# Two accumulator tiles instead of one, and an earlier place in the order for weight blocks, in a hybrid decoder trunk

## The chip, the cores and the metric

The kernel runs on one core of one Trainium2 chip. A core has five engines that each work through a queue of their own in order: TensorE (PE) multiplies 128-row blocks and writes PSUM, VectorE (DVE) and ScalarE (ACT) do elementwise work and read PSUM, GpSimd (POOL) and SyncE (SP) mostly issue transfers. They wait for each other by semaphores. The metric is the device time of one launch in microseconds. Three runs of the kernel before took 1014.68 to 1016.35 us, with a median of 1015.87.

## The reference

Input is a sequence of 512 tokens with 1024 channels, in front of which 16 learned tokens are put (528 positions). One layer is computed:

```
u    = rmsnorm(h) * mix_norm_w
proj = u @ w_in              # pool input, z, xBC, dt, two gates
y_pool = pool_mixer(u_pool) @ w_pool_up
xBC  = silu(causal_conv4(xBC))          # x: 2048, B and C: 8 groups x 128
dt   = softplus(dt + dt_bias);  a = -exp(a_log)
y    = ssd_chunked(x, dt, a, B, C) + x * d_skip      # chunks of 128 positions
y    = group_rmsnorm(y * silu(z)) * ssd_norm_w;  y_ssd = y @ w_ssd_out
h    = h + (gate_pool * y_pool + gate_ssd * y_ssd) @ w_o
h    = h + relu(rmsnorm(h) @ w_ff1)**2 @ w_ff2
out  = rmsnorm(h)[:, 16:]
```

The scan has 32 heads of 64 channels in 8 groups. In ssd_chunked a group's positions are cut into chunks; inside a chunk y is (C B^T, masked and multiplied by exp of differences of the summed decay) times x dt, between chunks a 128x64 state per head is carried on.

## The kernel before

All products are in float32, made of three products of split operands: a number is stored as a rounded part (hi) and the rest (lo), and hi·hi, hi·lo and lo·hi are summed in PSUM. A weight block is 128x1024 floats, which is eight 128x128 tiles. block() (L115) takes tiles for it, issues the load on SP's queue (L95) into one of three raw buffers, the cast to hi on ACT (L111) and the subtraction that gives lo on DVE (L113). There are four buffers each for hi (whi) and lo (wlo); a cast waits until the matmuls that read the block four places earlier are through with its buffer. A cast and a subtraction of a full block take about 1.05 and 1.2 us.

The scan goes over the groups 0 to 7. For group g, group_proj (L529) computes the projections of B, C, two halves of x and two halves of z from u, each as eight weight tiles with 16 high and 8 low matmuls per half of the positions (proj, L207; the results are the PSUM tiles px, and pz for z), and then a convolution of four taps (conv, L433: first tap on ACT L436, the others on DVE L439, silu on ACT L441). ssd (L590) computes the scan of the group before it, interleaved with these: transposes to ptb, ptm, ptx (L605 to L618); exps of the decay on ACT (eb, L632; abc, L637, L643, L644); C B^T in pcb (L655); states in pst, copied to st0 (L666) and carried on by DVE (L671, L672); the mask multiply on DVE (L675); then po (L684) from the states and py (L690) from the chunk itself, summed by DVE to yt (L693 to L697), normed by png, rs and a reciprocal (L708 to L713). A gate block (pgp) comes with some groups.

In groups 4 to 7 the two halves of x are computed together by pair() (L492), which uses seven products of half the size instead of eight: b11, b21, t2, t1, s3, b22, t4 in this order, each of 12 matmuls of 128 rows by 264 positions (8 with hi, 4 with lo weights, L505 and L508). Their operands are blocks whip and wlop from pair_operands (L471), two products to a block, and sums of u (t0h, t0l, t1h, t1l, made by L919 and L920). The products accumulate in two banks: b11, t2, s3, t4 in bank 0, b21, t1, b22 in bank 1. After each product its bank is read out to rax or rbx, by ACT (L510 b11, L515 t2, L517 t1, L524 t4) or by DVE (L512 b21, L520 s3, L522 b22), and the next product in that bank may write it when this is done.

PSUM has eight banks of 128x512 floats. Pool psa has two buffers of two banks each (psum2, L192), pool psb four of one bank (psum1, L195), in which ptb, ptm, ptx, pcb, pst, po, py and png of the scan take turns.

After the scan come its output projection, the pooling branch, w_o and the MLP (from about 690 us on), none of whose code is touched.

What sets the order of the work is a scheduler: the program is written as generators that are woven together (weave, L728), each instruction has a priority by its place in the program, and the scheduler puts each engine's queue in an order by priority among what it takes to be ready. tc.issue_after adds an order between two instructions. tc.high_priority(n) gives what is issued under it the priority of a place n instructions sooner.

Of the kernel before, what the change touches and what calls it, by code (L numbers as in the profile page):

```python
# [19 lines left out]
HALF = L // 2  # L20
# [44 lines left out]
def kernel(ctx: ExitStack, tc, xT, x, w, fx, f1, f2, vec, fnw, out):  # L65
# [15 lines left out]
    def raw_tile(name):  # L81
        nraw[0] += 1
        if scan_raw and nraw[0] % 4 == 0:
            return scan_raw[0].tile([P, 1024], F32, tag="raw", name=name)
        return wp.tile([P, 1024], F32, tag="raw", name=name, bufs=3)

    def block_tiles():
        b = nblk[0]
        nblk[0] += 1
        return (b, raw_tile(f"raw{b}"),  # L90
                wp.tile([P, 1024], F32R, tag="whi", name=f"whi{b}"),
                wp.tile([P, 1024], F32R, tag="wlo", name=f"wlo{b}"))

    def block_load(t, c):
        nc.sync.dma_start(t[1][:, c], w[t[0], :, c])  # L95
# [5 lines left out]
    def after(*ins):  # L101
        st = ExitStack()
        for i in ins:
            if i is not None:
                st.enter_context(tc.issue_after(i.ins))
        return st

    def block_split(t, c, behind=None, cast_behind=None):
        b, raw, hi, lo = t
        with after(cast_behind):  # L110
            act.copy(hi[:, c], raw[:, c])  # L111
        with tc.issue_after(behind.ins) if behind is not None else nullcontext():
            dve.tensor_tensor(lo[:, c], raw[:, c], hi[:, c].bitcast(F32), op=ALU.subtract)  # L113

    def block(behind=None, cast_behind=None):  # L115
        t = block_tiles()
        block_load(t, slice(0, 1024))
        block_split(t, slice(0, 1024), behind, cast_behind)
        return t[2:]

    def raw_block():
# [13 lines left out]
    def units():  # L135

        while True:
            hi, lo = block()
            for j in range(NK):
                yield hi[:, j * P : (j + 1) * P], lo[:, j * P : (j + 1) * P]  # L140
# [51 lines left out]
    def psum2(name):  # L192
        return psa.tile([P, 1024], F32, tag="mm", name=name)

    def psum1(name):  # L195
        return psb.tile([P, 512], F32, tag="s", name=name)
# [155 lines left out]
    for i in range(2):  # L352
        pb = psum1(f"pb1_{i}")
        c = slice(3 * i, 3 * i + 3)
# [35 lines left out]
    for c in (slice(0, P), slice(P, W)):  # L390
        n = c.stop - c.start
# [67 lines left out]
    def factor_u(name):  # L459
        if name in ("A11", "A12", "A22"):  # L460
            o = 0 if name == "A11" else 4
            c = HF[1] if name == "A22" else HF[0]
            return [(uh[o + k][:, c], ul[o + k][:, c]) for k in range(4)]
        n, c = {"S1": ("1", HF[1]), "S2": ("0", HF[0]), "S3": ("0", HF[1]), "S4": ("1", HF[0])}[name]
        return [(T[n, "h", k][:, c], T[n, "l", k][:, c]) for k in range(4)]
# [5 lines left out]
    def pair_operands(i):  # L471

        s, h = divmod(i, 2)
        q = {"b11": B11, "b22": B22, "b21": B21}
        for a in range(0, 7, 2):
            ms = [m[0] for m in MULTIPLY[a : a + 2]]
            n = nblk[1]
            nblk[1] += 1
            raw = raw_tile(f"rawp{n}")
            hi = wp.tile([P, 1024], F32R, tag="whi", name=f"whip{n}")  # L480
            lo = wp.tile([P, 1024], F32R, tag="wlo", name=f"wlop{n}")
            for j, m in enumerate(ms):
                src = fx[s, q[m]] if m in q else wsum["fx", s, m]
                nc.sync.dma_start(raw[:, 512 * j : 512 * (j + 1)], src[:, 512 * h : 512 * (h + 1)])
            c = slice(0, 512 * len(ms))
            block_split((n, raw, hi, lo), c)
            for j in range(len(ms)):
                yield hi[:, 512 * j : 512 * (j + 1)], lo[:, 512 * j : 512 * (j + 1)]

# [1 line left out]

    def pair(kind, g, r):  # L492

        ps = psum2(f"pq{kind}{g}")
        banks = (ps[:, :HALF], ps[:, 512 : 512 + HALF])
        operands = pair_operands(PAIRS.index((kind, g)))
        one, two = HF
        for m, f, n, start, stop in MULTIPLY:
            o = banks[n]
            wt = next(operands)  # L500
            f = factor_u(f)
            for low in range(2):
                for k in range(4):
                    wk = wt[low][:, k * P : (k + 1) * P]
                    at = pe.matmul(o, wk, f[k][0], start=start and not low and k == 0,  # L505
                                   stop=stop and low == 1 and k == 3, skip_group_check=True)
                    if not low:
                        pe.matmul(o, wk, f[k][1], start=False, stop=False, skip_group_check=True)  # L508
            if m == "b11":
                act.copy(r[0][:, one], o)  # L510
            elif m == "b21":
                dve.tensor_tensor(r[0][:, one], r[0][:, one], o, op=ALU.add)  # L512
            elif m == "t2":
                second_product[g] = at
                act.activation(r[1][:, one], o, AF.Copy, scale=-1.0)  # L515
            elif m == "t1":
                act.copy(r[1][:, two], o)  # L517
                yield
            elif m == "s3":
                dve.tensor_tensor(r[1][:, two], r[1][:, two], o, op=ALU.subtract)  # L520
            elif m == "b22":
                dve.tensor_tensor(r[1][:, one], r[1][:, one], o, op=ALU.add)  # L522
            else:
                act.copy(r[0][:, two], o)  # L524
# [4 lines left out]
    def group_proj(g, cur, gate=None):  # L529
# [4 lines left out]
        def plain(dst, t, skip):  # L534
            if first and (dst is bt or dst is ct):
                view = viewB if dst is bt else viewC
            else:
                runs, view = wide(psum2(f"px{g}_{t}"), skip)
                proj(runs, block(), X if first else U)
            conv(dst, first_raw(t, view, skip) if first else view, t)  # L540

        def z_half(ps, i):

            with tc.issue_after(done[0].ins) if g == 1 else nullcontext():
                wt = block(None, halved.get(g - 1) if gate is not None else None)
            proj(narrow(ps), wt, X if first else U, None if i else second_product.get(g))
# [4 lines left out]
        for kind, ts, paired in (("b", bcs, both), ("x", xs, g in X_PAIRS)):  # L551
            if paired:
                r = raw_pair(kind, g)
                yield from pair(kind, g, r)
                for (dst, t, skip), src in zip(ts, r):
                    conv(dst, src[:, skip:], t)
                yield
            else:
                for t in ts:
                    plain(*t)  # L560
                    filled.setdefault(g - 1, mm[0])
                    yield
            if both:
                i = 0 if kind == "b" else 1
                ps = psum2(f"pz{g}_{i}")[:, :SEQ]
                z_half(ps, i)
                z_ready[g] = act.activation(zt[:, i, :], ps, AF.Silu)
                yield
# [481 lines left out]
    for d in range(NK):  # L1050
        ps = psum1(f"psl{d}")
# [108 lines left out]
    for n, d in enumerate(MERGE):  # L1160
# [9 lines left out]
        ps = psum2(f"pup{d}")[:, :SEQ]  # L1170
# [389 lines left out]
    for c in range(NC - 1):  # L1560
        z, e = c == 0, c == NC - 2

        n = 2 * c + 3
# [63 lines left out]
    c = NC - 1  # L1627
# [14 lines left out]
    for t in range(4):  # L1642
        T, st = t // 2, slice((t % 2) * P, (t % 2 + 1) * P)
        n = 0
        for half in range(2):
            parts = [(0, 512)] if half == 0 or t < 3 else [(0, 256), (256, 256)]
            for a, m in parts:
                ps = p2v[t] if T == 0 and half == 0 else lastp[:, 512:] if a else (
                    lastp[:, :512] if (t, half) == (3, 0) else psum1(f"pl{t}_{half}"))
                ps = ps[:, a : a + m]  # L1650
# [5 lines left out]
                for k, seg in ((1, (A11, 3)[T]), (0, (A12, A22)[T])):  # L1656
                    wh, wl = wq[k, half]
                    for p in range(2):
                        x0 = p * 512 + a
                        f = i == 0 and not (T == 0 and half == 0) and not a  # L1660
# [170 lines left out]
```

## Time and profile before

| | |
|---|---|
| median of three runs | 1015.87 us (1014.68 to 1016.35) |
| the profiled execution | 1013.97 us |
| its span, first to last instruction | 1012.3 us |
| TensorE busy | 992.1 us, 98% of the span |
| VectorE, ScalarE, GpSimd busy | 804.3, 604.9, 122.7 us |
| mean granted TensorE clock | 0.996 of full speed |

How to read its views: the page gives the busy time of each engine and, in 40 slices of 25.3 us, its share in tenths and the granted clock. The view of waits sums for each group of instructions how long its engine stood idle ahead of it and what ended that. The timeline lists the instructions of an engine: start, time that it or its run of like instructions took, engine, line, operation, output <- inputs by the program's names (numbers left out, so px is px3_19 or another), shapes, the count of the run, and in brackets the idle time ahead of it with its releaser. Matmuls are pipelined, so a matmul of 0.28 us may start 0.12 us after the one before it.

### The profile page before, as it was taken

What the parts mean: (1) busy time and instruction counts of PE and PEld (TensorE: products, weight loads), DVE (VectorE), ACT (ScalarE), POOL (GpSimd) and SP (SyncE); (2) the same over time, 40 slices, a digit from 0 to 9 for tenths busy, and PEclk for the clock granted to TensorE, in tenths of its full rate; (3) what the DMA queues carried; (4) which work ended last, traced back from release to release, by engine and by line L of the source; (5) the groups of instructions that cost most, each with busy time, mean ns of one, the idle gap of its engine ahead of it and who ended that gap; (6) DMA issues with size and microseconds to landing.
All of it is one profiled execution on the core that took longest, in us unless ns stands there. A gap on an engine that the chain in (4) does not pass through costs nothing.

```text
span 1012.3 us, 15679 instructions
## 1 busy us (share of the span) xinstructions
PE 992.1 (98%) x6035; PEld 874.9 (86%) x6035; DVE 804.3 (79%) x1162; ACT 604.9 (60%) x856; POOL 122.7 (12%) x215
## 2 busy tenths in 40 slices
PE   9999997999999999999999999999999999999997
PEld 7889996988888898987899888887889999999986
DVE  7968896869853788978789657876988878888885
ACT  8657848395943666675445434367656656665654
POOL 0001221211112213213300000221000000000000
PEclk9999998999999999999999999999999999999999
DMA  7274877676889758587823631989354464554432
GB/s 255 85 259 128 252 217 188 180 196 189 232 244 262 207 147 255 137 264 156 270 84 124 230 125 62 288 199 337 91 187 150 142 195 138 166 172 151 137 105 84
DMA packets 61803, 184.52 MB, mean 182 GB/s; under 512 B 7072, under 2 KB 8416, under 8 KB 60704
## 3 DMA queue, kind: packets, MB, share of 16 engines
q1 hardware_dynamic: 39456, 109.00, 32.4%
q0 software_dynamic: 18240, 67.51, 26.1%
q10 hardware_dynamic: 4032, 7.00, 1.9%
q8 instruction: 47, 0.77, 0.3%
q14 instruction: 28, 0.23, 0.1%
HBM read 173.13 MB, written 58.59 MB: 229 GB/s over the span
## 4 chain that ended last, share of the span: by engine, by line
PE 90%; ACT 5%; DVE 2%; DMA 2%; issue 1%; ACTq 0%; DVEq 0%
PE px L1450 8%; PE px L214 7%; PE alpha L1518 6%; PE pz L214 6%; PE px L1453 4%; PE px L217 4%; PE alpha L1521 3%; PE pgp L214 3%; PE pz L217 3%; PE pgs L214 3%; PE pqx L505 3%; DMA raw<-in_w 2%; PE pso L145 1%; PE pgp L217 1%; PE pso L146 1%; PE pso L148 1%
## 5 line engine op out<-in xcount | busy, mean ns | idle before, releaser
L113 DVE TENSOR_TENSOR wlo<-raw,whi 128x1024 fp32r<-128x1024 f32 (+2 forms) x88 | 101.7, 1170 | 43.7 <-ACT whi L111 25.7
L111 ACT CAST whi<-raw 128x1024 fp32r<-128x1024 f32 (+2 forms) x88 | 87.5, 1010 | 74.8 <-DMA raw<-in_w 17.8
L214 PE MATMUL px<-uh,whi 128*128 128x264 f32 (+1 forms) x320 | 82.4, 295 | 5.7 <-ACT whi L111 5.7
L217 PE MATMUL px<-ul,whi 128*128 128x264 f32 (+1 forms) x320 | 79.9, 287 | 0.0
L214 PEld LDWEIGHTS px<-uh,whi 128*128 128x128 f32 x320 | 61.5, 192 | 7.1 <-ACT whi L111 6.0
L1225 DVE TENSOR_TENSOR ht<-ht,alpha 128x1024 f32<-128x1024 f32 x35 | 42.7, 1219 | 29.1 <-PE alpha L1518 29.1
L217 PEld LDWEIGHTS px<-ul,whi 128*128 128x128 f32 x320 | 61.3, 192 | 0.2
L1148 ACT CAST shi<-rawf 128x1024 fp32r<-128x1024 f32 x42 | 44.2, 1053 | 28.6 <-PE alpha L1521 18.2
L1518 PE MATMUL alpha<-shi,hh 128*128 128x512 f32 x140 | 55.2, 394 | 0.0
L1521 PE MATMUL alpha<-shi,hl 128*128 128x512 f32 x140 | 54.7, 391 | 0.0
L1149 DVE TENSOR_TENSOR slo<-rawf,shi 128x1024 fp32r<-128x1024 f32 x42 | 51.2, 1218 | 0.6 <-ACT shi L1148 0.6
L1453 PE MATMUL px<-vsl,shi 128*128 128x256 f32 x192 | 47.4, 280 | 0.0
L1450 PE MATMUL px<-vsh,shi 128*128 128x256 f32 x192 | 47.4, 281 | 0.0
L214 PE MATMUL pz<-uh,whi 128*128 128x512 f32 x112 | 43.9, 392 | 0.0
L217 PE MATMUL pz<-ul,whi 128*128 128x512 f32 x112 | 43.7, 390 | 0.0
L214 PE MATMUL px<-uh,wlo 128*128 128x264 f32 (+1 forms) x320 | 41.8, 283 | 0.0
L214 PEld LDWEIGHTS px<-uh,wlo 128*128 128x128 f32 x320 | 39.9, 188 | 0.0
L1518 PE MATMUL alpha<-slo,hh 128*128 128x512 f32 x140 | 37.4, 389 | 0.0
L1450 PEld LDWEIGHTS px<-vsh,shi 128*128 128x128 f32 x192 | 36.2, 188 | 0.9
L1453 PEld LDWEIGHTS px<-vsl,shi 128*128 128x128 f32 x192 | 36.1, 188 | 0.9
L1453 PE MATMUL px<-vl,shi 128*128 128x256 f32 x144 | 36.1, 283 | 0.0
L713 DVE RECIPROCAL rs<-rs 128x128 f32<-128x128 f32 x32 | 27.2, 911 | 11.1 <-ACT rs L711 10.9
(593 smaller groups left out, 3079.2 us busy)
## 6 DMA issues: line engine op xcount, KB each, us to landing
raw<-in_w SPq DMA_DIRECT2D x96, 512.0 KB, 4.7
f_t<-in_f POOLq DMA_DIRECT2D x38, 512.0 KB, 6.9
f_s<-in_f POOLq DMA_DIRECT2D x26, 512.0 KB, 6.6
b<-in_f SPq DMA_DIRECT2D x21, 512.0 KB, 4.5
rawf<-in_f SPq DMA_DIRECT2D x36, 256.0 KB, 3.0
rawf<-f_t SPq DMA_DIRECT2D x36, 256.0 KB, 3.2
abc<-acs_d POOLq DMA_DIRECT2D x8, 1024.0 KB, 6.5
f_t<-f_t POOLq DMA_DIRECT2D x12, 512.0 KB, 6.7
```

Of the source, the lines that this page charges most:

```text
L111: act.copy(hi[:, c], raw[:, c])
L113: dve.tensor_tensor(lo[:, c], raw[:, c], hi[:, c].bitcast(F32), op=ALU.subtract)
L214: pe.matmul(o, wt, rhs[0][k][:, c], start=part == 0 and k == 0, stop=part == 1 and k == NK - 1)
L217: mm[0] = pe.matmul(o, wt, rhs[1][k][:, c], start=False, stop=False)
L505: at = pe.matmul(o, wk, f[k][0], start=start and not low and k == 0, stop=stop and low == 1 and k == 3, skip_group_check=True)
L1148: splits.append((act.copy(hi, src), dve.tensor_tensor(lo, src, hi.bitcast(F32), op=ALU.subtract)))
L1149: dve.tensor_tensor(lo, src, hi.bitcast(F32), op=ALU.subtract)))
L1225: added[0] = dve.tensor_tensor(o, o, src, op=op)
L1450: pe.matmul(ps, m, f[k][0], start=start and not low and k == 0, stop=stop and low == 1 and k == 3, skip_group_check=True)
L1453: pe.matmul(ps, m, f[k][1], start=False, stop=False, skip_group_check=True)
L1518: pe.matmul(ps[t], hh[:, p, seg, st], m, start=bool(first and not low and p == 0), stop=bool(last and low and p == 1), skip_group_check=True)
L1521: pe.matmul(ps[t], hl[:, p, seg, st], m, start=False, stop=False, skip_group_check=True)
```

## The change

Two edits. In block() the load and the split, and in pair_operands the split, are issued under tc.high_priority(100). In pair() bank 1 is no longer the second half of the psa tile but a psb tile of its own, pox4 to pox7; pqx4 to pqx7 stays the psa tile, of which the second bank now lies unused. No instruction is added or removed but for one table load of ACT, which falls away.

```diff
     def block(behind=None, cast_behind=None):
         t = block_tiles()
-        block_load(t, slice(0, 1024))
-        block_split(t, slice(0, 1024), behind, cast_behind)
+        with tc.high_priority(100):
+            block_load(t, slice(0, 1024))
+            block_split(t, slice(0, 1024), behind, cast_behind)
         return t[2:]
...
             c = slice(0, 512 * len(ms))
-            block_split((n, raw, hi, lo), c)
+            with tc.high_priority(100):
+                block_split((n, raw, hi, lo), c)
...
     def pair(kind, g, r):
 
-        ps = psum2(f"pq{kind}{g}")
-        banks = (ps[:, :HALF], ps[:, 512 : 512 + HALF])
+        banks = (psum2(f"pq{kind}{g}")[:, :HALF], psum1(f"po{kind}{g}")[:, :HALF])
```

Line numbers up to L116 are the same in both kernels, and those of the changed kernel are one greater from there to pair() and behind it. The order of SP's loads changes in one place only (two blocks of w_o, one place later each). ACT and DVE change in many places. Here are three, each with the line numbers of its own kernel; the text keeps to those of before.

ACT, between group 1's norm and the first block of group 3 (whi24 is the cast of the block for group 3's B, px3_19; abc2, eb2, zt2 and btok2 belong to group 2's scan). Before:

```order
L583 ACT_TABLE_LOAD
L583 ACTIVATE zt2_1406<-pz2_1837 128x1024
L607 COPY btok2_1916<-ptb2_1918 128x512
L637 ACTIVATE abc2_1913<-abc2_1913,dtok_84 128x128
L644 ACT_TABLE_LOAD
L644 ACTIVATE abc2_1913<-abc2_1913 128x1024
L643 ACTIVATE abc2_1913<-abc2_1913 128x1024
L111 COPY whi24_1967<-raw24_1966 128x1024
L111 COPY whi25_2058<-raw25_2057 128x1024
L111 COPY whi26_2143<-raw26_2142 128x1024
L111 COPY whi27_2229<-raw27_2228 128x1024
```

And now:

```order
L712 ACTIVATE rs1_1829<-png1_1826,eps_80 128x512
L758 DMA gate_d4_139<-gp4_1821 128x512
L111 COPY whi24_1967<-raw24_1966 128x1024
L111 COPY whi25_2058<-raw25_2057 128x1024
L633 ACT_TABLE_LOAD
L633 ACTIVATE eb2_1942<-abc2_1913 64x1024 x2
L721 COPY yh1_0_1900<-yt1_1612 128x512
L721 COPY yh1_1_1905<-yt1_1612 128x512
L584 ACT_TABLE_LOAD
L584 ACTIVATE zt2_1406<-pz2_1837 128x1024
L608 COPY btok2_1916<-ptb2_1918 128x512
```

The casts of blocks 24 and 25 stood behind group 2's exps (L643, L644) and stand ahead of its first ones (eb2).

PE, in the pair of group 4 (po3 and py3 belong to group 3's scan; whip0 and wlop0 hold the operands of b11 and b21). Before:

```order
L684 MATMUL po3_0_2629<-ct3_1911,st3_3_2543 128x128
L505 MATMUL pqx4_2651<-uh2_96,wlop0_2654 128x264
L505 MATMUL pqx4_2651<-uh3_97,wlop0_2654 128x264
L684 MATMUL po3_1_2718<-ct3_1911,st0_3_2540 128x128
L684 MATMUL po3_1_2718<-ct3_1911,st1_3_2541 128x128
L684 MATMUL po3_1_2718<-ct3_1911,st2_3_2542 128x128
L684 MATMUL po3_1_2718<-ct3_1911,st3_3_2543 128x128
L690 MATMUL py3_1_2723<-abc3_2419,xdt3_2421 64x128 x8
L505 MATMUL pqx4_2651<-uh4_98,whip0_2653 128x264
L508 MATMUL pqx4_2651<-ul4_106,whip0_2653 128x264
```

And now:

```order
L506 MATMUL pqx4_2651<-uh2_96,wlop0_2655 128x264
L506 MATMUL pqx4_2651<-uh3_97,wlop0_2655 128x264
L685 MATMUL po3_0_2629<-ct3_1911,st3_3_2543 128x128
L506 MATMUL pox4_2652<-uh4_98,whip0_2654 128x264
L509 MATMUL pox4_2652<-ul4_106,whip0_2654 128x264
L506 MATMUL pox4_2652<-uh5_99,whip0_2654 128x264
L509 MATMUL pox4_2652<-ul5_107,whip0_2654 128x264
L506 MATMUL pox4_2652<-uh6_100,whip0_2654 128x264
```

The product b21, which wrote pqx4 behind po3_1 and py3_1, writes pox4 and follows b11 with one matmul of po3_0 between; po3_1 and py3_1 come behind it.

DVE, at the pair of group 5 (ct5 is the convolution of group 5's C, yt4 and yl4 are group 4's result, rax5 takes up b21). Before:

```order
L439 TENSOR_SCALAR ct5_2930<-px5_29_3418,vs_82,ct5_2930 128x512
L717 TENSOR_SCALAR yt4_3153<-yt4_3153,vs_82,rs4_3410 128x512
L439 TENSOR_SCALAR ct5_2930<-px5_29_3418,vs_82,ct5_2930 128x512
L717 TENSOR_SCALAR yt4_3153<-yt4_3153,vs_82,rs4_3410 128x512
L439 TENSOR_SCALAR ct5_2930<-px5_29_3418,vs_82,ct5_2930 128x512
L512 TENSOR_TENSOR rax5_3478<-rax5_3478,pqx5_3480 128x264
L721 TENSOR_TENSOR yl4_0_3551<-yt4_3153,yh4_0_3550 128x512
L721 TENSOR_TENSOR yl4_1_3556<-yt4_3153,yh4_1_3555 128x512
```

And now:

```order
L440 TENSOR_SCALAR ct5_2931<-px5_29_3419,vs_82,ct5_2931 128x512
L718 TENSOR_SCALAR yt4_3154<-yt4_3154,vs_82,rs4_3411 128x512
L440 TENSOR_SCALAR ct5_2931<-px5_29_3419,vs_82,ct5_2931 128x512
L513 TENSOR_TENSOR rax5_3479<-rax5_3479,pox5_3482 128x264
L440 TENSOR_SCALAR ct5_2931<-px5_29_3419,vs_82,ct5_2931 128x512
L113 TENSOR_TENSOR wlo46_3630<-raw46_3628,whi46_3629 128x1024
L722 TENSOR_TENSOR yl4_0_3553<-yt4_3154,yh4_0_3552 128x512
```

The read of b21 (L512 before, L513 now) has moved ahead of the last step of ct5 and of the second scaling of yt4.

## The prediction

> **What bounds the kernel.** I read the page first: its span, the busy line of its first part and the clock row of its second.
> ```profile
> span 1012.3 us, 15679 instructions
> ...
> PE 992.1 (98%) x6035; PEld 874.9 (86%) x6035; DVE 804.3 (79%) x1162; ACT 604.9 (60%) x856; POOL 122.7 (12%) x215
> ...
> PEclk9999998999999999999999999999999999999999
> ```
> TensorE (PE) is busy for 992.1 of 1012.3 us, so 20.2 us of idle time are all that a change of order can win directly; the matmuls, their shapes and their number stay. The clock row has one digit below 9, the seventh. The second view is the waits of PE by releaser (in total, times, longest):
> ```profile
> PE px L214 <- ACT whi L111: 5.7, 1, 5.7
> ...
> PE pqx L505 <- DVE rax L512: 1.5, 1, 1.5
> PE psp L145 <- ACT sp L867: 1.4, 1, 1.4
> PE pqx L505 <- ACT rax L510: 1.4, 1, 1.4
> PE po L684 <- DVE st L672: 0.9, 1, 0.9
> PE pgp L214 <- ACT whi L111: 0.6, 1, 0.6
> ...
> PE py L690 <- issue: 0.4, 1, 0.4
> ```
> The largest is one wait for the cast of a weight block; two belong to the pairs' products (pqx). These are the places the change can reach, and each I looked up in the timeline. First PE around 171 us, with a view of two windows behind it (us, PE busy, granted clock, DMA share, GB/s):
> ```profile
> 164.48 1.04 PE L618 MATMUL ptx<-ident,xc 128*128 128x128 f32 x8
> 171.25 0.59 PE L214 MATMUL px<-uh,whi 128*128 128x264 f32 x1 [5.73 <-ACT whi L111]
> ```
> ```profile
> 171.25:176.75 5.50, 5.50 (x32) 0.70 0.60 178
> 181.11:185.14 4.03, 4.03 (x35) 1.00 0.46 130
> ```
> PE has finished the transposes of group 2 at 165.52 and stands still until 171.25. The 32 matmuls of the high half of block 24 then take 5.50 us at a granted clock of 0.70, where the same 32 of block 25 take 4.03 at 1.00: the stall costs 5.73 and, behind it, 1.47 of clock. What ACT and DVE did meanwhile:
> ```profile
> 156.09 0.69 ACT L711 ACTIVATE rs<-png,eps 128x512 f32<-128x512 f32 x1
> 156.80 1.28 ACT L632 ACT_TABLE_LOAD   x1
> 158.09 2.15 ACT L632 ACTIVATE eb<-abc 64x1024 f32<-64x1024 f32 x2
> ...
> 169.22 1.04 ACT L643 ACTIVATE abc<-abc 128x1024 f32<-128x1024 f32 x1
> 170.17 3.87 ACT L111 CAST whi<-raw 128x1024 fp32r<-128x1024 f32 x4
> ```
> ```profile
> 156.82 3.39 DVE L713 RECIPROCAL rs<-rs 128x128 f32<-128x128 f32 x4 [2.82 <-ACT rs L711]
> ...
> 171.23 4.63 DVE L113 TENSOR_TENSOR wlo<-raw,whi 128x1024 fp32r<-128x1024 f32 x4 [3.83 <-ACT whi L111]
> ```
> ACT was not idle and the data were not late: it worked through group 2's decay (L632 to L644) and then did four casts in one go. It is an order of work, not a lack of it.
>
> **The change part by part.** Term 1, the priority, at this place. The new ACT order puts the casts of blocks 24 and 25 right behind the square root of 156.09, ahead of the table load of 156.80. With 0.97 us for one cast (3.87 by 4) block 24 is ready at about 157.8, 7.7 us before PE asks at 165.52. Its low part stands on DVE behind the reciprocals (done at 160.21) and takes 1.16 (4.63 by 4), so about 161.4, against a need at 165.52 + 4.03 = 169.5. The wait of 5.73 goes, and with it the cause of the 1.47. What is late next: eb and everything behind it on ACT by two casts, and the exps of L643/L644 by a third one (block 26), 2.9 us, so to about 173.1 instead of 170.26. The mask multiply behind them (L675, 2.28 us in a row below) ends near 175.6. PE needs it at group 2's py:
> ```profile
> 188.05 1.09 PE L690 MATMUL py<-abc,xdt 128*64 128x128 f32 x16
> ```
> Seven microseconds sooner that is about 180.8, so there are 5.2 us to spare, and I book nothing. Term 1: −7.2.
>
> [...]
>
> Term 2, the same priority at groups 0 to 1, where ACT and DVE rows read:
> ```profile
> 83.60 1.04 ACT L643 ACTIVATE abc<-abc 128x1024 f32<-128x1024 f32 x1
> ...
> 85.23 0.35 ACT L666 COPY st<-pst 128x256 f32<-128x256 f32 x1
> ```
> ```profile
> 86.28 0.38 PE L684 MATMUL po<-ct,st 128*128 128x128 f32 x2
> ```
> PE lost 0.41 (py, issue) and 0.87 (po, for st) there. In the new order PE does 29 matmuls of the next block's product before po and py (29 × 0.126, which is 4.03 by 32, = 3.7 us), so it comes to po at 86.28 + 3.7 = 89.9. But ACT now does the convolution of bt, for which it must wait, ahead of the decay, which I count as 3 us on the exps (84.64 becomes 87.6), and a table load (1.28 as above) and bt's silu (0.63, like ct's in term 4) ahead of the copy to st: 87.6 + 1.28 + 0.63 + 0.35 = 89.9 instead of 85.58. That is level with PE. The chain of st1 behind it, two DVE steps of 0.41 less the py matmuls in between, can cost 0.5. I take −1.28 + 0.48 = −0.8; the ends are −1.28 and +1.0 (ACT another 1.5 us late).
>
> Term 3, at the first po of group 1, where no wait was:
> ```profile
> 128.56 2.28 DVE L675 TENSOR_TENSOR abc<-abc,cbm 128x2048 f32<-128x2048 f32 x1
> 130.76 0.41 DVE L672 TENSOR_TENSOR st<-st,pst 128x256 f32<-128x256 f32 x1
> ```
> ```profile
> 130.86 0.85 PE L684 MATMUL po<-ct,st 128*128 128x128 f32 x4
> ```
> PE reaches it at 130.86, and the state that its second matmul needs ends at 131.17 behind the mask multiply. Arriving 0.8 us sooner with DVE's order unchanged there, it waits about 0.5. Term 3: +0.5 (0 to 0.8, since it can give back at most term 2).
>
> Term 4, the bank of its own, in group 4. ACT and PE:
> ```profile
> 240.11 0.63 ACT L441 ACTIVATE ct<-ct 128x512 f32<-128x512 f32 x1 [3.65 <-DVE ct L439]
> 240.65 0.61 ACT L919 CAST t0h<-rau 128x528 fp32r<-128x528 f32 x1
> ...
> 242.09 0.38 ACT L510 COPY rax<-pqx 128x264 f32<-128x264 f32 x1
> 243.82 1.05 ACT L111 CAST whi<-raw 128x1024 fp32r<-128x1024 f32 x1 [1.35 <-PE pqx L508]
> ```
> ```profile
> 242.53 0.39 PE L505 MATMUL pqx<-uh,whip 128*128 128x264 f32 x1 [1.40 <-ACT rax L510]
> ...
> 244.92 0.50 PE L214 MATMUL pgp<-uh,whi 128*128 128x512 f32 x1 [0.65 <-ACT whi L111]
> ```
> The second product (b21) writes the other bank, yet waited until the copy of the first had read its own, because both were one tile; ACT came to that copy late, behind ct's silu and the casts of t0h and t1h. With a tile of its own b21 needs no copy and follows the first product directly, po and py then cover the copy: −1.40. The cast at 243.82 waited for b21's high half to free its slot; that half is now done over 4 us sooner and the cast runs under po and py: −0.65. Term 4: −2.05.
>
> Term 5, group 5: DVE and PE.
> ```profile
> 337.68 0.74 DVE L439 SCALAR_TENSOR_TENSOR ct<-px,vs,ct 128x512 f32<-128x512 f32 x1
> 338.34 0.42 DVE L512 TENSOR_TENSOR rax<-rax,pqx 128x264 f32<-128x264 f32 x1
> ```
> ```profile
> 333.47 0.28 PE L505 MATMUL pqx<-uh,whip 128*128 128x264 f32 x1
> ...
> 334.94 0.49 PE L605 MATMUL ptb<-ident,bt 128*128 128x128 f32 x3
> ...
> 338.81 0.39 PE L505 MATMUL pqx<-t0h,whip 128*128 128x264 f32 x1 [1.50 <-DVE rax L512]
> ```
> The third product (t2, bank 0) waited for DVE's read of bank 1, behind a queue of L439 and L717. In a tile of its own bank 0 asks only for the ACT copy, long done; bank 1's next product (t1) comes 1.47 us later (a product, from 333.47 to 334.94), at 337.9, and L512 has moved ahead of one L439 and one L717, so it ends near 337.5. Term 5: −1.50.
>
> Term 6, what the split costs. The seven products now alternate between the tiles, mostly with no other matmuls between, where z's matmuls stood in the gaps before. An eviction costs PE 0.47 from its start (338.34 to 338.81), and a product covers 1.47, so it is free if ACT or DVE is free within a microsecond of the end. They aren't always: a cast (1.05) or a low part (1.16) queued ahead of an eviction uses that up. In group 5 the last product would be ready at 342.77 by my count of DVE's queue and is wanted at 342.75. The bounds are 0 and, with one eviction stuck behind a cast and a low part in each of four pairs (1.05 + 1.16 + 0.47 − 1.47 = 1.2 us), +4.8. The margins I counted lie near zero and above, so nearer the low end: +0.9. The extra tile takes one of psb's four buffers for the length of a pair; the scan's po and py there wait for no buffer in the new order as I traced it, and if they did, the price is the wait for one DVE read, inside that bound.
>
> The wait at psp (1.43), the start (1.5) and the rest keep their order and I book nothing.
>
> Sum: −7.2 − 0.8 + 0.5 − 2.05 − 1.5 + 0.9 = −10.15. The profiled run took 1013.97 us, so 1003.8 by it; that run is 1.9 below the median of 1015.87, which puts the forecast for the median at 1005.7. Less than 0.2% of this kernel, 2 us, can't be told from nothing.
>
> **The rivals.** *A remnant* (0.12): ACT or DVE reaches blocks 24 and 25 later than I counted, for example because the cast stands behind something whose input is late, and about 2 us of idleness plus the 1.47 of clock stay. That leaves 3.5 of the 7.2 and gives 1009.2. Against it: 7.7 us of room for the cast.
>
> *The pairs pay* (0.14): term 6 is at its upper bound, as every pair loses its z fillers. Then 1005.7 + 3.9 = 1009.6. For it: margins near zero in group 5. Against it: groups 6 and 7 show no wait at all before.
>
> *The stall moves* (0.06): the exps, three casts later, hold the mask multiply, and PE stops at py instead of at px. It needs the mask 5.2 us later than counted to begin, and 5.2 + 7.2 to cancel term 1 with its clock loss; the rest of the gains then pay the misses: no change.
>
> *Casts ahead of evictions* (0.12, slower). The page's groups have for the casts (busy, mean ns, idle before):
> ```profile
> L111 ACT CAST whi<-raw 128x1024 fp32r<-128x1024 f32 (+2 forms) x88 | 87.5, 1010 | 74.8 <-DMA raw<-in_w 17.8
> ```
> ACT already stands idle 74.8 us in front of casts whose slot or data aren't there, and its queue is in order: a cast moved forward to such a place holds the evictions and convolutions behind it, and PE waits for those. It is one mechanism over all the scan's blocks. Groups 1 to 7 have 45 plain blocks (11 to 55) and 16 of pairs; over these 61 it cancels the gain of 11.05 (the sum without term 6) at 0.18 us each, and at 0.25 it gives 15.3 − 11.05 = 4.2 more than the median, 1020.1. For it: the bt convolution and the cast stand ahead of group 0's decay now. Against it: in all of before PE waited for ACT evictions only the 1.40 of group 4, though ACT stood in front of casts just so.
>
> **How the numbers follow.** My sum has 0.56; its own range is 1002.5 to 1008.5 (term 6 from 0 to 3, term 2 to its end, and a spread of a microsecond between runs). Remnant and paying pairs, both faster, make 0.26, so faster is 0.82, no change 0.06, slower 0.12. The range of 1001.5 to 1012.5 takes in the first three cases and leaves out the last two and a small tail below.
>
> **What the profile would show.** Right: no wait of px for whi L111 above 1 us, and the seventh clock digit a 9; PE idle near 10 us; no wait of pqx for L510 or L512. Wrong: a wait of pqx or pox above 1 us in three or more pairs (term 6), a wait of py for abc L675 near 180 us, or ACT rows of L111 with more idle time in front than 74.8 us and PE waiting for L436 or L666.

## The result, and the profile after

The changed kernel takes 1002.95 us (median of four runs, 1002.25 to 1004.41) beside 1015.27 us for the kernel before: a ratio of 0.9885, 95% interval 0.9872 to 0.9899. It is 12.3 us faster. The forecast was 1005.7, 10.2 below the median it started from, with a range of 1001.5 to 1012.5. Measured again beside other kernels the ratio was 0.9881 (0.9865 to 0.9898). The profiled executions differ by less (1013.97 and 1003.26 us, 10.7 apart), and the account below is of those.

The page of the changed kernel, the same lines as of before:

```profile
span 1001.6 us, 15673 instructions
...
PE 989.0 (99%) x6035; PEld 873.4 (87%) x6035; DVE 804.2 (80%) x1162; ACT 602.9 (60%) x855; POOL 121.9 (12%) x215
...
PEclk9999999999999999999999999999999999999999
```

TensorE's idle time fell from 20.2 to 12.6 us (near 10 was forecast), and its busy time by another 3.1, although it does the same 6035 matmuls. Its waits, the six longest:

```profile
PE pz L215 <- DVE xc L440: 1.7, 1, 1.7
PE pdt L260 <- DVE ones_r L157: 1.5, 1, 1.5
PE psp L146 <- ACT sp L868: 1.4, 1, 1.4
PE alpha L1519 <- DVE ht L1226: 0.6, 1, 0.6
PE pz L998 <- ACT pu L1010: 0.4, 1, 0.4
PE pxx L998 <- ACT pu L1008: 0.3, 1, 0.3
```

No wait of px for a cast and none of pqx is left; the first row is new. The place of the old stall in the timelines of ACT, DVE and PE (each its own view):

```profile
157.88 0.69 ACT L712 ACTIVATE rs<-png,eps 128x512 f32<-128x512 f32 x1
158.47 1.99 ACT L111 CAST whi<-raw 128x1024 fp32r<-128x1024 f32 x2
160.47 1.28 ACT L633 ACT_TABLE_LOAD   x1
...
173.46 1.04 ACT L645 ACTIVATE abc<-abc 128x1024 f32<-128x1024 f32 x1
```

```profile
161.91 1.16 DVE L113 TENSOR_TENSOR wlo<-raw,whi 128x1024 fp32r<-128x1024 f32 x1
...
174.53 2.29 DVE L676 TENSOR_TENSOR abc<-abc,cbm 128x2048 f32<-128x2048 f32 x1 [0.31 <-ACT abc L645]
```

```profile
165.73 1.04 PE L619 MATMUL ptx<-ident,xc 128*128 128x128 f32 x8
166.53 0.37 PE L215 MATMUL px<-uh,whi 128*128 128x264 f32 x1
...
181.36 0.87 PE L691 MATMUL py<-abc,xdt 128*64 128x128 f32 x10
```

The two casts are done at 160.46, six microseconds before TensorE wants the first, and px follows the transposes without a gap. What was pushed back, the exps and the mask multiply, ends at 176.82, 4.5 us ahead of py.

To see where every microsecond went, I paired the matmuls of two traces by their place in the program and took, for the end of some PSUM tiles, how much earlier or later they come. The steps between such ends, in us, after less before (a minus is a gain):

```
stretch (up to the last matmul of ...)    whole  banks  24-27  block() both   24-27   17-56
                                         change alone  alone  alone  prior. +banks  +banks
start            (gate block 3)           0.34   0.19   0.18  -0.30  -0.31   0.32   0.25
groups 0 to 1    (png0)                   1.28  -0.51   0.17   1.24   1.30  -0.53   0.17
groups 1 to 2    (ptx2)                  -0.37  -0.07   0.33  -0.37  -0.37  -0.07   0.85
stall and clock  (px3_19)                -7.49   0.36  -7.49  -7.49  -7.49  -7.49  -7.49
groups 2 to 3    (px4_28)                 0.58   0.00   0.31   0.58   0.58   0.31   0.05
pair of group 4  (pz4)                   -1.99  -2.60   0.96   0.62   0.24  -2.62  -2.01
pair of group 5  (ptx5)                  -2.56  -2.50  -0.02  -0.27   2.66  -2.55  -2.57
pair of group 6  (png5)                  -0.81  -0.79   0.03   0.06   0.02  -0.78  -0.81
pair of group 7  (png6)                  -0.21  -0.68   0.00   0.09   0.51  -0.68  -0.18
pooling branch   (pup0)                   0.71   0.06  -0.36   0.56   0.94   0.17   0.61
w_o              (last pf)               -1.17  -0.83  -0.71  -1.13  -1.15  -0.27   0.17
MLP              (end)                    0.96   0.03   0.04   0.01   0.05   0.05   0.01
```

The first column is the changed kernel; the others are the experiments that follow: the banks' edit alone, the priority for blocks 24 to 27 alone, for all of block() alone, both priorities without the banks' edit, and the banks' edit with the priority for fewer blocks.

### The profile page after: what moved, and what is told of

The parts are those of the page before. It is cut to its first block, busy times and chain, and to the rows that moved or that the text cites. A ratio compares the mean times of both kernels' runs of the same rounds, so it can differ in the third digit from the quotient of the medians.

```text
span 1001.6 us, 15673 instructions
## 1 busy us (share of the span) xinstructions
PE 989.0 (99%) x6035; PEld 873.4 (87%) x6035; DVE 804.2 (80%) x1162; ACT 602.9 (60%) x855; POOL 121.9 (12%) x215
## 4 chain that ended last, share of the span: by engine, by line
PE 84%; DVE 7%; ACT 4%; DMA 3%; issue 1%; SPq 0%; ACTq 0%; DVEq 0%
PE px L1451 8%; PE px L215 7%; PE alpha L1519 6%; PE pz L215 6%; PE px L1454 4%; PE px L218 4%; PE pgp L215 3%; PE alpha L1522 3%; PE pz L218 3%; PE pgs L215 3%; DMA raw<-in_w 2%; PE pqx L506 2%; PE py L691 2%; PE pgp L218 2%; PE pso L146 1%; PE wo_alpha L1213 1%
## 5 line engine op out<-in xcount | busy, mean ns | idle before, releaser
L113 DVE TENSOR_TENSOR wlo<-raw,whi 128x1024 fp32r<-128x1024 f32 (+2 forms) x88 | 102.2, 1171 | 45.0 <-ACT whi L111 29.7
L1451 PE MATMUL px<-vh,shi 128*128 128x256 f32 x144 | 36.0, 282 | 0.0
```

The lines of the kernel that those rows point to most:

```text
L1451: pe.matmul(ps, m, f[k][0], start=start and not low and k == 0, stop=stop and low == 1 and k == 3, skip_group_check=True)
```

## The experiments

**The two edits apart.** First the banks' edit alone:

```diff
-        ps = psum2(f"pq{kind}{g}")
-        banks = (ps[:, :HALF], ps[:, 512 : 512 + HALF])
+        banks = (psum2(f"pq{kind}{g}")[:, :HALF], psum1(f"po{kind}{g}")[:, :HALF])
```

> The change with the banks' edit alone, no priority. If the two parts add (theory A): the wait of 5.7 us of px for the cast of block 24 and the clock of 0.83 stay, the waits of pqx for L510 and L512 and of pgp for its cast go, and so does the time that the interleaved products cost: about 5.5 us faster than before (2.0, 2.5, 0.8 and 0.2 in groups 4 to 7, as the two traces differ), ratio 0.9945. If the pairs need the earlier casts for products that follow each other directly (theory B): new waits of pqx or pox for whip or an eviction, and less than 3 us faster.

Measured: 1007.7 us, ratio 0.9933 (0.9911 to 0.9955), so 6.9 us where about 5.5 were expected. The four pairs give 2.60, 2.50, 0.79 and 0.68, together 6.6 us, and none of it needs a cast to come earlier; theory B falls in this point. The largest wait is the old one:

```profile
PE px L214 <- ACT whi L111: 5.8, 1, 5.8
```

Then the priorities alone, with one tile for both banks:

```diff
+        with tc.high_priority(100):
+            block_load(t, slice(0, 1024))
+            block_split(t, slice(0, 1024), behind, cast_behind)
...
+            with tc.high_priority(100):
+                block_split((n, raw, hi, lo), c)
```

> The change with both priorities and one tile for both banks. Theory A: px waits for no cast and the clock stays at full speed (-7.5), pz1 waits 1.7 us for xc (+1.3 net at groups 0 to 1), and the waits of pqx for L510 and L512 stay: 5 to 6 us faster than before, ratio 0.9945. Theory B: the earlier casts alone also take the waits of the pairs, and this kernel is as fast as the whole change, 12 us faster than before.

Measured: 1011.13 us, ratio 0.9961 (0.9948 to 0.9975), so 3.4 us where theory A wanted 5 to 6. It missed because the priority does harm in the pair of group 5 that the banks' edit hides. PE and DVE there:

```profile
333.90 0.39 PE L507 MATMUL pqx<-t0h,whip 128*128 128x264 f32 x1 [2.64 <-DVE rax L514]
```

```profile
331.63 0.74 DVE L440 SCALAR_TENSOR_TENSOR ct<-px,vs,ct 128x512 f32<-128x512 f32 x1
332.30 1.21 DVE L113 TENSOR_TENSOR wlo<-raw,whi 128x1024 fp32r<-128x1024 f32 x1
333.43 0.42 DVE L514 TENSOR_TENSOR rax<-rax,pqx 128x264 f32<-128x264 f32 x1
```

A low part (1.21) now stands in front of the read of b21, so t2's wait grew from 1.50 to 2.64, and the clock behind it fell to 0.50 for 3.3 us (windows in the last section). With bank 1 in a tile of its own, bank 0 doesn't wait for that read, and in the whole change's order the read stands ahead of that low part as well, so the whole change is free of this. In this pair the two parts are thus not additive: the columns give −2.50 and +2.66 alone and −2.56 together. Over the whole kernel 6.9 and 3.4 make 10.3 where the change is worth 12.3, but the intervals are too wide to tell these apart.

To see whether that one low part is the cause, block()'s priority without the one in pair_operands, whose order has the read first again:

> Block()'s priority alone, the banks and pair_operands as in before. With both priorities and one tile DVE made the low part of block 46 ahead of L512, and the wait there grew from 1.5 to 2.6 us with half the clock behind it. Here the order has L512 first. If that one low part is the cause: the wait of pqx for L512 is at most 1.6 us, the clock stays at 1.00 behind it, and the run is 2 to 3 us faster than the one with both priorities (about 6 us faster than before, ratio 0.994). If something else held DVE: the wait stays above 2 us.

Measured: 1007.76 us, ratio 0.9921 (0.9904 to 0.9937), by the traces 3.4 us faster than with both priorities, by the ratios 4, a little more than the 2 to 3 expected; 2.9 of it is in the pair of group 5. The wait is back at 1.50, and the first matmuls behind it start 0.12 us apart from the second on, without the steps of 0.22 that the kernel with both priorities has at the clock of 0.50:

```profile
332.80 0.39 PE L506 MATMUL pqx<-t0h,whip 128*128 128x264 f32 x1 [1.50 <-DVE rax L513]
```

**The priority in its places.** Only for the blocks of the stall:

```diff
+        with tc.high_priority(100) if 24 <= t[0] <= 27 else nullcontext():
```

> Before with the priority for blocks 24 to 27 only, the banks as in before. If the wait for block 24 and its clock are worth 7.2 us by themselves, as term 1 has it, and the banks' gain lies on top: 7 to 7.5 us faster than before, ratio 0.993, with the waits of pqx for L510 (1.4) and L512 (1.5) as in before; its ratio times that of the banks alone (0.9933) is that of both together (0.985 to 0.986). If the two depend on each other: less than 6 us, or more than 9.

Measured: 1007.4 us, ratio 0.9916 (0.9901 to 0.9931), 8.6 us by the medians and 6.6 by the trace, one above and one below the 7 to 7.5 expected; the place itself gives 7.49, as in every kernel with this priority there. 0.9916 times 0.9933 is 0.985. A cost came too, since the pair of group 4 was met at another moment, and its wait for the ACT copy grew from 1.40 to 2.33:

```profile
236.98 0.39 PE L506 MATMUL pqx<-uh,whip 128*128 128x264 f32 x1 [2.33 <-ACT rax L511]
```

The same with the banks' edit:

> The banks' edit, and the priority for blocks 24 to 27 only (group 3's B, C and x). If the priority is worth something at this one place only and costs elsewhere (theory A): the wait for block 24 is gone as in the whole change, the waits of 0.4 and 0.9 us at groups 0 to 1 of before are back, pz1's 1.7 us and the loss of 0.7 us in the pooling branch are gone: 1 to 2 us faster than the whole change, so 13 to 14 us faster than before, ratio 0.987. If the priority of the other blocks carries the gain in the pairs (theory B): 3 us or more slower than the whole change.

Measured: 1000.14 us, ratio 0.9858 (0.9836 to 0.988). The whole change and this kernel once more, measured side by side:

> The changed kernel again, beside the next one on the same chip. Both theories: ratio 0.9885 to before, as measured.

> The banks' edit with the priority for blocks 24 to 27 only, again. If the 2 to 3 us by which its trace is shorter than that of the whole change are its own and not a run's: median 2 to 3.5 us below that of the whole change in the same call, ratio 0.985 to 0.986. If they are scatter: within 1 us of it.

Measured: 1002.65 us (1002.02 to 1004.71) and 1000.05 us (999.27 to 1000.43), ratios 0.9881 (0.9865 to 0.9898) and 0.9849 (0.9834 to 0.9864). This kernel beats the whole change. The two sets of runs do not overlap, and the two intervals only just do not. The columns say where its 2.6 us are: 1.8 at groups 0 to 1, 0.6 and 0.5 in the pairs of groups 4 and 7, 0.5 in the pooling branch, with 0.3 to 0.9 given back at w_o. Priority for the other blocks costs more than it brings.

Does it cost by group 1's blocks and the pooling branch alone?

```diff
-        with tc.high_priority(100):
+        with tc.high_priority(100) if 17 <= t[0] <= 56 else nullcontext():
```

> The whole change, but with block()'s priority for blocks 17 to 56 only, so not for group 1's and not for those of the pooling branch and behind. Theory A: the wait of pz1 and the pooling branch's loss are gone as with blocks 24 to 27 alone, 1 to 2 us faster than the whole change, ratio 0.987, and within 1 us of the kernel with blocks 24 to 27. Theory B: the same as the whole change within 1 us, as the pairs' blocks have their priority.

Measured: 1001.3 us, ratio 0.9865 (0.9841 to 0.9889), between the two, and 1.2 us above the kernel with blocks 24 to 27 (1000.14) where at most 1 was expected. pz1's wait is gone as expected. The first row below is the old wait of po at group 0; the second is py at group 1, which also runs in two pieces there, 6 and 10 matmuls that take 1.35 us where 16 in one piece take 1.02. This wait and the pieces are the 0.85 lost at groups 1 to 2:

```profile
PE po L685 <- DVE st L673: 0.9, 1, 0.9
PE py L691 <- issue: 0.5, 1, 0.5
```

The pooling branch still loses 0.61, but not where the whole change does. Of ACT's queue there, before and in the whole change:

```profile
550.24 0.38 ACT L1007 ACTIVATE pu<-pxx 128x264 f32<-128x264 f32 x1
550.52 1.04 ACT L111 CAST whi<-raw 128x1024 fp32r<-128x1024 f32 x1
```

```profile
539.47 1.05 ACT L111 CAST whi<-raw 128x1024 fp32r<-128x1024 f32 x1
540.42 0.38 ACT L1008 ACTIVATE pu<-pxx 128x264 f32<-128x264 f32 x1
```

In the whole change a cast of block() has moved ahead of a copy out of PSUM, and pxx waits 0.33 us for that copy, 0.6 with what follows. This wait is in all six profiles with priority for every block and in none of the other six (the kernel with blocks 17 to 56 is one of these). That kernel loses its 0.61 at pz some 55 us sooner: pz waits 1.05 instead of 0.45 for another copy of pu (L1009), which stands behind a cast in before too, but ACT waits 2.18 instead of 1.57 us for that cast's load. Why the load comes later was not followed.

**How much of the stall is the clock.** Two kernels bring the stall back in part, by an order between the cast of block 24 and an ACT instruction:

```diff
-            block_split(t, slice(0, 1024), behind, cast_behind)
+            block_split(t, slice(0, 1024), behind, z_ready[2] if t[0] == 24 else cast_behind)
```

> The whole change, but the cast of block 24 comes behind the silu of zt2, so that TensorE stands idle some 1.7 us in front of px3_19, right behind 1.7 us of transposes. If only idleness lowers the clock, and 1.7 us is too short: the 32 high matmuls take 4.0 us at a clock of 1.00, the run is 1.7 us longer than the whole change. If the transposes count as idle time: 5 us or more for the 32 matmuls, the clock below 0.85 in them, and 3.2 us longer.

> The whole change, but the cast of block 24 comes behind the first of group 2's two exps, idle time of TensorE about 4.8 us. Both theories: the clock falls as in before, the 32 high matmuls take 5.2 to 5.6 us and the run is 6 to 6.5 us longer than the whole change.

(The second has done.get(2), the first of the exps to be issued, in the place of z_ready[2].) PE of the first, and the windows of the 32 high matmuls in both (us, PE busy, granted clock, DMA share, GB/s):

```profile
167.87 0.39 PE L215 MATMUL px<-uh,whi 128*128 128x264 f32 x1 [1.61 <-ACT whi L111]
```

```profile
167.87:171.88 4.01, 4.01 (x32) 1.00 1.01 253
```

```profile
171.87:177.10 5.23, 5.23 (x32) 0.73 0.59 181
```

With 1.61 us of idleness behind 1.7 us of transposes the 32 matmuls take 4.01 us at a clock of 1.00, and the stretch loses 1.9 us against the changed kernel; with 5.30 us they take 5.23 at 0.73 and it loses 6.8. So the clock's share of term 1 (1.47 us in before) is a cost of its own, which the remnant of 1.61 us did not have. The whole times, 1006.21 and 1012.22 us in one run each, are 3.6 and 9.6 above the changed kernel measured beside them, more than expected: the first trace has a wait of 1.81 us at the start of the MLP with a clock of 0.50 for 3.3 us behind it (3.4 us together), and the second lost the clock at psp (0.65 from 454 to 456 us and 0.50 from 456 to 458; 1.6 us) and waited at alpha (1.1 with what follows).

## Why the prediction was right, and where not

Term 1 was right in mechanism and size: −7.2 forecast, −7.49 measured at the place, in six kernels alike. The displaced exps and mask multiply kept 4.5 of the 5.2 us counted. Not counted was 0.58 behind it: py2 and po2 now run in pieces between each other, without a wait. In two pieces of 10 and 6 py's matmuls take 1.38 us, in one piece of 16 they took 1.03; the kernel with blocks 17 to 56 has py2 in one piece, and 0.05 in this stretch.

Term 2 had the wrong sign. The waits of 0.41 and 0.87 did go, and ACT's copy to st ended at 90.21 (89.9 forecast), but the stretch lost 1.28 instead of gaining 0.8. The step that failed is that I followed the late ACT chain only to po and py. DVE has more behind it: the taps of the x convolution that read px1_2, a tile that fills one of psa's two buffers, which pz1 is to have. Before, the last of them started at

```profile
101.01 0.75 DVE L439 SCALAR_TENSOR_TENSOR xc<-px,vs,xc 128x525 f32<-128x525 f32 x1
```

with 1.9 us to spare until pz1 at 103.62. Now DVE and PE read:

```profile
95.90 1.22 DVE L113 TENSOR_TENSOR wlo<-raw,whi 128x1024 fp32r<-128x1024 f32 x1
...
101.14 0.76 DVE L440 SCALAR_TENSOR_TENSOR xc<-px,vs,xc 128x527 f32<-128x527 f32 x1
101.82 1.22 DVE L113 TENSOR_TENSOR wlo<-raw,whi 128x1024 fp32r<-128x1024 f32 x1
102.95 0.76 DVE L440 SCALAR_TENSOR_TENSOR xc<-px,vs,xc 128x526 f32<-128x526 f32 x1
103.63 0.68 DVE L694 TENSOR_TENSOR yt<-po,eb 128x512 f32<-128x512 f32 x1
104.23 0.76 DVE L440 SCALAR_TENSOR_TENSOR xc<-px,vs,xc 128x525 f32<-128x525 f32 x1
```

```profile
105.13 0.47 PE L215 MATMUL pz<-uh,whi 128*128 128x512 f32 x1 [1.69 <-DVE xc L440]
```

px1_2 was complete at 95.28 and is given free at 104.99, 3.2 us later than before. Two low parts (L113, blocks 15 and 16) stood behind these taps and now stand ahead of the last, 2.4 us; the rest is the chain of st, which DVE begins at 90.24 instead of 87.56, less the taps of bt that it then no longer has to do. The waits alone are only 0.41 of the 1.28 (1.69 less the 0.41 and 0.87 that went). The other 0.9 is busy time, about half of it because po and py run in more pieces. The low parts ahead of the taps are the mechanism of the slower rival, work on weight blocks ahead of a read of PSUM, on DVE instead of ACT and at one place instead of everywhere: 1.69 us, not 0.18 at each of 61 blocks. The cast ahead of the copy pu in the pooling branch (above) is a second such place, on ACT as the rival had it. Against that rival the prediction said that in all of before PE waited for ACT evictions only the 1.40 of group 4; its own second view has 1.43 at psp for ACT's copy L867 too.

Term 3 (+0.5) did not come, −0.37: TensorE reached group 1's po 1.5 us later than before, not 0.8 sooner, so the state was there. It hung on term 2.

Term 4 was right in its two waits, which are gone, but that −1.99 was measured for −2.05 forecast is partly luck: the banks' edit alone gave −2.60 there, 0.55 more than the waits, and the priorities take 0.6 back.

Terms 5 and 6 have to be taken together. For the waits of group 5 I forecast −1.50, for the four pairs' evictions a cost of +0.9; the pairs of groups 5, 6 and 7 gave −2.56, −0.81 and −0.21. No eviction made TensorE wait. The zero margin that I counted in group 5 held, here DVE's reads and PE's last product:

```profile
334.50 0.42 DVE L521 TENSOR_TENSOR rbx<-rbx,pqx 128x264 f32<-128x264 f32 x1
```

```profile
335.03 0.34 PE L506 MATMUL pqx<-uh,whip 128*128 128x264 f32 x1
```

So term 6 has the wrong sign, and what I missed is that z's matmuls between the products were not free cover. Before, at the change from z's matmuls of 512 columns to a product's of 264 (start and duration; the next start tells how long a matmul holds the array):

```profile
343.50 0.39 PE L217 MATMUL pz<-ul,whi 128*128 128x512 f32 x1
343.72 0.35 PE L505 MATMUL pqx<-t0h,whip 128*128 128x264 f32 x1
343.91 0.28 PE L508 MATMUL pqx<-t0l,whip 128*128 128x264 f32 x1
344.03 0.29 PE L505 MATMUL pqx<-t0h,whip 128*128 128x264 f32 x1
```

The first matmul behind a change of width holds it for 0.19 us here, the next for 0.12. A change of tile alone costs nothing here: where a product in pox follows one in pqx directly, or the other way, the first matmul takes 0.12 too (17 places in the changed kernel). Over the pair of group 6, which has no wait in either kernel, from each matmul's start to the next one's:

```
                              before            after
first of 264 columns       8 x 0.203 us      4 x 0.217 us
others of 264             76 x 0.123        80 x 0.122
first of 512               5 x 0.251         1 x 0.228
others of 512             43 x 0.227        47 x 0.227
of 128 columns            26 x 0.095        26 x 0.079
all                       24.47 us          23.54 us
```

Of the 0.93 us, 0.4 is in the matmuls of 128 columns (po and py, mostly since py now runs in one piece), the rest in fewer changes. It shows as busy time, not as a wait, which is why no view of waits had it. What makes a first matmul longer the traces do not tell.

Of the rivals, a remnant of the stall, paying pairs and a stall that moves were all absent. That about 2 us of idleness would keep the 1.47 us of clock was my estimate, which no run at this place shows: behind 1.61 us the clock stayed at 1.00. The loss of 0.71 in the pooling branch and the gain of 1.17 at w_o were not forecast. The gain is a wait of before that is gone: pf waits 0.29 for DVE's vl (L1254) and is about 1 us late three matmuls on. Of the other profiles only the one with blocks 17 to 56 has such a wait (0.44), and it alone gains nothing there; why it goes was not followed. The 0.96 at the MLP is a wait of 0.55 at alpha with the rest behind it in one profile; the same kernel's second profile has 0.02. The terms come to −10.15, the two profiles of the changed kernel to −10.71 and −11.71 and the medians to −12.3: the spread between executions is as large as the smaller terms, and part of it is the clock (below). That the sum came within 0.6 us of the profile is in part luck. Term 2 was 2.1 too hopeful, and stretches outside the terms lost 2.6; terms 3, 5 and 6 together did 3.9 better than forecast, term 1 did 0.3 better and w_o gained 1.2.

## What to carry to other kernels

Look for the one place where an engine with work to do did it in the wrong order, and raise the priority there; raised everywhere, the same edit took back 2.6 us of what it brought, in part since it also put casts and low parts ahead of reads of PSUM. When a chain is pushed back on ACT or DVE, follow it to the last read of every PSUM tile that it delays, since the next user of that buffer waits for it (pz1 here, 1.69 us). Two accumulators in one tile made one bank's matmuls wait for the other bank's read (1.40 and 1.50 us in before, neither with a tile each); and matmuls of another width put between as cover cost about 0.08 us at each change back in the pair of group 6 (0.203 us against 0.123), so products that can follow each other should.

## What the runs showed of the hardware

The clock fell behind much shorter waits than the 5.73 us of the stall, and not each time. Behind 2.64 us of idleness in the kernel with both priorities and one tile (the window of the wait, the first matmuls, the next 3.3 us, and what follows; us, PE busy, granted clock, DMA share, GB/s):

```profile
331.26:333.90 2.64, 0.00 (x1) 1.00 1.07 313
333.90:334.50 0.60, 0.60 (x5) 0.98 0.96 191
334.50:337.80 3.30, 3.30 (x15) 0.50 1.05 253
337.80:341.00 3.20, 3.20 (x23) 0.99 1.01 259
```

TensorE worked again for 0.60 us at a clock of 0.98, then for 3.30 at 0.50. The same came behind 1.81 us (the first kernel with part of the stall, at alpha: 1.13 us at 1.00, then 3.30 at 0.50), and behind the 1.4 to 1.5 us at psp in the second kernel with part of the stall (the two windows above) and in one of the two profiles with the banks' edit and blocks 24 to 27. The other of these has the same wait and a mean clock of 0.999 instead of 0.997; before and the changed kernel have it too (1.43 and 1.44) and kept 1.00 in the 3.4 us behind it. The one that lost it:

```profile
442.77:443.90 1.13, 1.13 (x5) 0.99 0.00 0
443.90:447.20 3.30, 3.30 (x21) 0.50 0.93 111
```

Behind the 2.33 us above the matmuls start 0.12 us apart from the second on, as they do at a clock of 1.00. Behind the 1.69 at pz1 the changed kernel kept 1.00 for the next 6.7 us, and the two other kernels of the table with this wait lose no more in that stretch, 1.24 and 1.30 beside 1.28. So a wait between 1.4 and 2.6 us here cost itself, and sometimes 1.6 us more, half of the 3.3. In the stall of before the clock fell while TensorE still stood idle, 2.2 us after its last matmul (1.00 until 167.7, 0.50 from 168.5 on, the first matmul at 171.25), and in the second kernel with part of the stall 4.7 us after it, as far as the mean of 0.94 from 166 to 172 us tells. Why it falls then, and why the same wait loses it once and not another time, the runs do not show. Whether transposes count as idle time stays open: 1.61 us behind 1.7 us of transposes kept the clock at 1.00, but the 1.69 at pz1 did so too.
